# The end of a one-core decoder block: last 512 columns of each side in halves, and one block of the last side scaled by ScalarE and added to residual rows in the output

## The chip, the cores and the metric

The kernel runs on one core of a Trainium2 chip. The metric is the device time of one execution in microseconds (us); the time of a kernel is the median over its runs. A profiled execution gives a span (from the first to the last instruction of the program) and a trace of every engine: PE (TensorE, matmuls; PEld is its weight load), DVE (VectorE), ACT (ScalarE), POOL (GpSimd) and SP (SyncE, which here only issues transfers).

## The reference

One decoder layer over 256 rows of 2048 columns in float32: a mixer (dilated attention and a gated recurrence, not touched here), then a feed-forward part. The end of it is what matters:

```python
h = h + rmsnorm(y @ w_mix_out[layer], norm_mix_post[layer])
a = rmsnorm(h, norm_ffn_pre[layer])
gt, up = jnp.split(a @ w_ffn_gate_up[layer], [D_FF], axis=-1)
ff = (jax.nn.silu(gt) * up) @ w_ffn_down[layer]      # (256, 5632) @ (5632, 2048)
h = h + rmsnorm(ff, norm_ffn_post[layer])
return h
```

The last line needs the mean square of a whole row of ff (2048 columns) before any column of that row can be scaled; the scaled row is then added to h, the residual.

## The kernel before, in words

**Tiling.** The 256 rows are two sides of 128 rows (i = 0, 1; `ov` at line 720 is the output as partition, side, column). The 2048 output columns are four blocks of 512 (j = 0 to 3). The down projection runs as two `Wide` blocks of 1024 columns: the first gives j = 0, 1 and the second, `blocks[-1]`, gives j = 2, 3. Each has 22 steps of 256 rows of the weight. A float32 product is made of three float32r matmuls (high by high, high by low, low by high), all recorded at line 171. In some steps a 2 by 2 block of products is made of seven instead of eight; for that, transfers prepare sums of weights, and `gather` (line 531) folds the banks of the seven into an SBUF tile of four quarters, `e` (`b.rest`), while the last steps go on.

**Order.** Nothing reorders the program: each engine executes its own instructions in the order in which the code emits them (`manual_schedule`), and a framework puts semaphore waits where one engine's instruction needs another's. Transfers are issued by SP (most weight loads, line 302), by POOL (accumulating ones, line 308) and by ACT. A step's weights are loaded, split into high and low parts by ACT (line 399) and DVE (line 407), and multiplied two steps later; SP's next load waits until a buffer is free. At step 6 of `blocks[-1]`, `h_back` (line 1502) has POOL load the residual columns of j = 0, 1, 2 back from memory (`h_t[0]` to `h_t[2]`); `h_t[3]` never left SBUF.

**The end.** The last three steps a, b, c (eight products each, no sevens) are multiplied in an order of their own (lines 1887 to 1897): side 0's j = 2 and 3, then side 1's j = 2 over a, b, c (18 matmuls of 512 columns), then side 1's j = 3 (18 more). After each of these four groups `finish(i, j)` emits

- `down_sum` (line 1614): DVE adds the PSUM bank to its quarter of `e`
- `down_square` (line 1619): ACT squares the quarter and leaves the row sum in a column of `fss`
- `down_gain` (line 1625): DVE multiplies the quarter by the row factor and the gain into `fz[j]`
- for j = 2, `so_far_of` (line 1643): three small DVE operations add the sums of j = 0, 1, 2
- for j = 3, `rsqrt_mean` (line 173: two small ACT and three small DVE operations give `r3`, the row's factor), and then `store` for j = 0 (in two pieces of 128 and 384 columns), 1, 2, 3: DVE makes `fz * r3 + h` (line 1666), and SP or ACT sends it to the output (line 1669).

DVE reads nothing of side 1 before it has stored side 0, since these five operations stand ahead in its order.

Of the kernel before, what the change touches and what calls it, by code (L numbers as in the profile page):

```python
# [16 lines left out]
AF = mybir.ActivationFunctionType  # L17
OP = mybir.AluOpType
# [93 lines left out]
def tile_hybrid_block(ctx: ExitStack, tc: tile.TileContext, t, out):  # L112
    nc = tc.nc
# [11 lines left out]
    def nm(s):  # L125
        serial[0] += 1
        return f"{s}_{serial[0]}"

    def rslot(s):
        return rpool.tile([P, 1024], F32R, tag="r", bufs=16, name=nm(s))  # L130
# [18 lines left out]
    def bank_of(n):  # L149
        return banks(n, 1).tile([P, 512], F32, tag=n, name=nm(n))  # L150

    def pair_of(n):
        return banks(n, 2).tile([P, 2, 512], F32, tag=n, name=nm(n))
# [7 lines left out]
    def p3(s, dtype, n, bufs, tag=None):  # L161
        return pool["now"].tile([P, n], dtype, tag=tag or s, bufs=bufs, name=nm(s))
# [4 lines left out]
    def small(s, n=8, bufs=6):  # L167
        return cpool.tile([P, n], F32, tag=f"small{n}", bufs=bufs, name=nm(s))

    def mm(ps, lhsT, rhs, start, stop):  # L170
        nc.tensor.matmul(ps, lhsT, rhs, start=start, stop=stop, skip_group_check=True)  # L171

    def rsqrt_mean(dst, ss, n, bias=None):

        w = ss.shape[-1]
        v, y, a = (small(s)[:, :w] for s in ("v", "y", "a"))
        bias = bias or (eps[:, 0:1], eps[:, 1:2])  # L180
        nc.scalar.activation(y, ss, AF.Ln, scale=1.0 / n, bias=bias[0])
        nc.scalar.activation(y, y, AF.Exp, scale=-0.5)
        nc.vector.tensor_scalar(v, ss, -0.5 / n, bias[1], op0=OP.mult, op1=OP.add)
        if w == 1:
            nc.vector.scalar_tensor_tensor(out=a, in0=y, scalar=v, in1=y, op0=OP.mult, op1=OP.mult)
        else:
            nc.vector.tensor_mul(a, y, y)
            nc.vector.tensor_mul(a, a, v)
        nc.vector.scalar_tensor_tensor(
            out=dst, in0=a, scalar=1.5, in1=y, op0=OP.add, op1=OP.mult  # L190
        )
# [35 lines left out]
    r2c = cpool.tile([P, 2], F32, name="r2c")  # L227
    r3c = cpool.tile([P, 2], F32, name="r3c")
# [7 lines left out]
    def ptile(s):  # L236
        n = {"early": 4, "middle": 5, "late": 2}[pool["name"]]
        return pool["now"].tile([P, 512], F32, tag="p", bufs=n, name=nm(s))
# [10 lines left out]
    blocks, seq, units, extra = [], [], [], []  # L249
# [221 lines left out]
                    going.remove(g)  # L471
            yield

    def multiply_wide(st, sides=(0, 1), groups=(0, 1)):
        b, i = st.block, st.i
        m, by7 = b.order[i]

        def prod(key, x, w, j, last=False):
            if key not in b.bank:
                side = "aux" if b.flip == (type(key) is not tuple) else "acc"  # L480
                if b.whole:
                    keys = next(k for k in PAIRS if key in k)
                    pair = b.bank[keys] = pair_of(side)
                    b.bank.update((k, pair[:, n, :]) for n, k in enumerate(keys))
                else:
                    b.bank[key] = bank_of(side)
            ps = b.bank[key]
            wh, wl = (v[:, j * 512 : (j + 1) * 512] for v in w)
            mm(ps, x[0], wh, key not in b.open, False)
            mm(ps, x[0], wl, False, False)  # L490
            mm(ps, x[1], wh, False, last)
            b.open.add(key)

        def act_of(s, k):
            return [x[:, s * P : (s + 1) * P] for x in b.xs(2 * m + k)[:2]]

        w = st.parts
        if not by7:
            for s in sides:
                for g in groups:  # L500
                    for k in range(2):
                        prod((s, g), act_of(s, k), w, 2 * g + k, st.last and k == 1)
            return
        w, d, sums = w[:2], w[2:], b.seven(m)
        last = i == b.last7

        go = {
            "o": lambda: prod((0, 1), act_of(0, 1), w, 3, st.last),
            "u": lambda: prod((0, 0), sums(3), w, 1, st.last),
            "t": lambda: prod((1, 1), act_of(1, 1), d, 2, st.last),  # L510
            "1": lambda: prod("p1", act_of(0, 0), w, 2, last),
            "6": lambda: prod("p6", sums(2), d, 0, last),
            "5": lambda: prod("p5", sums(1), d, 1, last),
            "7": lambda: prod("p7", sums(0), w, 0, last),
        }
        seven = [0 <= n < b.steps and b.order[n][1] for n in (i - 1, i + 1)]
        if i == 0:
            steps = "out1657"
        elif st.last:
            steps = "1765out" if seven[0] else "1657out"  # L520
        elif st.between:
            go["x"] = st.between() or (lambda: None)
            steps = "ou1x6t57"
        elif seven[0]:
            steps = "ou17t65"
        else:
            steps = "t65ou17" if seven[1] else "ou1657t"
        for x in steps:
            go[x]()
# [190 lines left out]
    ov = out[0].rearrange("(p b) c -> p b c", b=2)  # L720
# [532 lines left out]
    gates, bases = {}, {}  # L1253
# [32 lines left out]
    h_t, hT, y7 = {}, [], {}  # L1286
# [99 lines left out]
    def from_mix_to_ffn(n):  # L1386
# [41 lines left out]
        high()  # L1428
        mix_square(3, 1, m)
        base = so_far_of(zss[0], 1)  # L1430
        low()
        multiply(f0, (0,))
# [141 lines left out]
    fss, fz, fpost, parts_of, a7 = [], {}, [], {}, {}  # L1574

    def begin_down():
        fss.append(small("fss"))
        for j in range(2):
            fpost.append(rslot("fpost").bitcast(F32))
            nc.scalar.dma_start(  # L1580
                fpost[j],
                t["norm_ffn_post"][:, j * 1024 : (j + 1) * 1024].to_broadcast([P, 1024]),
            )
# [27 lines left out]
    def act(k):  # L1611
        return parts_of[k // 2](k % 2)

    def down_sum(j, i, b):

        f = b.rest[:, 2 * i + j % 2]
        nc.vector.tensor_add(f, b.bank[i, j % 2], f)

    def down_square(j, i, b):
        sq, r2 = fss[0][:, 4 * i + j : 4 * i + j + 1], r2c[:, i : i + 1]  # L1620
        nc.scalar.activation(  # L1621
            ptile("junk"), b.rest[:, 2 * i + j % 2], AF.Square, scale=r2, accum_out=sq
        )

    def down_gain(j, i, b):
        if i == 0:
            fz[j] = p3("fz", F32, 1024, 4, "so").rearrange("p (b c) -> p b c", b=2)
        nc.vector.scalar_tensor_tensor(
            out=fz[j][:, i, :], in0=b.rest[:, 2 * i + j % 2], scalar=r2c[:, i : i + 1],
            in1=fpost[j // 2][:, (j % 2) * 512 : (j % 2 + 1) * 512],  # L1630
            op0=OP.mult, op1=OP.mult,
        )

    def evac_down(b):
        parts = [(j, i) for i in range(2) for j in range(2)]
# [4 lines left out]
            down_gain(j, i, b)  # L1640
            yield

    def so_far_of(ss, i):

        b = small("base")
        nc.vector.tensor_reduce(
            b[:, 0:1], ss[:, 4 * i : 4 * i + 3], op=OP.add, axis=mybir.AxisListType.X
        )
        nc.vector.tensor_scalar(b[:, 0:1], b[:, 0:1], 1.0 / D, EPS, op0=OP.mult, op1=OP.add)
        nc.vector.tensor_scalar(b[:, 1:2], b[:, 0:1], -0.5, None, op0=OP.mult)  # L1650
        return b[:, 0:1], b[:, 1:2]

    def finish(i, j):

        b = blocks[-1]
        down_sum(j, i, b)
        down_square(j, i, b)
        down_gain(j, i, b)
        if j == 2:
            bases[i] = so_far_of(fss[0], i)  # L1660
            return
        sq, r3 = fss[0][:, 4 * i + 3 : 4 * i + 4], r3c[:, i : i + 1]

        def store(j, lo=0, hi=512, eng=nc.sync):
            z = fz[j][:, i, lo:hi]
            nc.vector.scalar_tensor_tensor(  # L1666
                out=z, in0=z, scalar=r3, in1=h_t[j][:, i, lo:hi], op0=OP.mult, op1=OP.add
            )
            eng.dma_start(ov[:, i, j * 512 + lo : j * 512 + hi], z)

        rsqrt_mean(r3, sq, D, bases[i])
        store(0, 0, 128)
        store(0, 128, 512, nc.scalar)
        store(1)
        store(2, eng=nc.scalar)
        store(3)


    w_in = t["w_in"][0]
# [69 lines left out]
    w = w_gu = t["w_ffn_gate_up"][0]  # L1749
# [31 lines left out]
    if len(H7) > 4:  # L1781
        first_j = [b for b in blocks if b.w is w_gu and type(b) is Wide][0]
        first_j.at[4] = more_sums
        blocks[-1].at[6] = h_back

    later = []

# [42 lines left out]
    for n, st in enumerate(seq):  # L1830
        b, i = st.block, st.i
# [55 lines left out]
    a, b, c = seq[-3:]  # L1887
    for g in range(2):
        for st in (a, b):
            multiply_wide(st, (0,), (g,))  # L1890
    for g in range(2):
        multiply_wide(c, (0,), (g,))
        finish(0, 2 + g)
    for g in range(2):
        for st in (a, b, c):
            multiply_wide(st, (1,), (g,))
        finish(1, 2 + g)


# [49 lines left out]
```

## Time and profile before

| | |
|---|---|
| median of 3 runs | 1674.45 us (1674.42 to 1674.69) |
| the profiled execution | 1675.0 us, its span 1673.2 us |
| PE busy | 1661.8 us, 99% of the span |
| DVE busy | 1477.7 us, 88% |
| ACT, POOL busy | 960.5 us (57%), 230.4 us (14%) |
| last matmul ends | 1664.6 us after the span's start |

PE is busy nearly throughout, so up to 1664.6 us the kernel lasts as long as its matmuls. The 8.6 us behind them belong to the last block's norm, the stores and their landing. Views used below: the page of the run; the chain of waits (what each piece of work waited for, followed back from the end); the groups of instructions by form; the timeline (one row for each instruction, or run of like ones: start, duration, engine, line); the busy time by windows; and the issues of transfers with their time from issue to landing.

### The profile page before, as it was taken

Reading aid. Unit: us, or ns where it says so; the run is one execution under the profiler, and the core shown is the slowest. Engines: PE = TensorE matmul, PEld = TensorE weight load, DVE = VectorE, ACT = ScalarE, POOL = GpSimd, SP = SyncE. Lnnn points to the kernel's source line nnn. Section 1 sums busy time; section 2 is a strip of 40 time slices with the busy share of each in tenths; the row PEclk is TensorE's granted clock in tenths of the full one; section 3 lists DMA queues with packets and bytes.
Section 4 is the critical chain, followed back from the end, with each engine's and each line's share of the span. In section 5 each row is a group of like instructions: output and inputs, shape, how many; then the busy total and the mean of one; then the engine's idle time right before and its main releaser. Section 6 shows DMA issues by size and latency. Waiting matters only on the chain.

```text
span 1673.2 us, 21505 instructions
## 1 busy us (share of the span) xinstructions
PE 1661.8 (99%) x8028; PEld 1390.4 (83%) x8028; DVE 1477.7 (88%) x1512; ACT 960.5 (57%) x959; POOL 230.4 (14%) x309
## 2 busy tenths in 40 slices
PE   9999999999999999999999999999999999999997
PEld 7888888888888888888888888888888888888886
DVE  6799999999987998867668888999999999899988
ACT  6566555565665444445445565666666666666664
POOL 0001111111003311313311010111111111000100
PEclk9999999999999999999999999999999999999999
DMA  8888888998769997969988857998988989887892
GB/s 283 268 261 258 269 244 264 277 289 274 234 204 316 313 268 219 279 209 303 297 249 250 279 187 245 274 277 273 282 280 268 283 268 278 255 256 236 258 307 103
DMA packets 235705, 436.56 MB, mean 261 GB/s; under 512 B 15408, under 2 KB 65632, under 8 KB 235600
## 3 DMA queue, kind: packets, MB, share of 16 engines
q1 hardware_dynamic: 195920, 345.94, 61.3%
q0 software_dynamic: 37056, 83.32, 22.7%
q10 hardware_dynamic: 2624, 5.92, 1.0%
q8 instruction: 63, 1.03, 0.3%
q14 instruction: 42, 0.34, 0.1%
HBM read 422.01 MB, written 52.43 MB: 284 GB/s over the span
## 4 chain that ended last, share of the span: by engine, by line
PE 93%; DVE 3%; DMA 2%; issue 1%; ACT 1%; SPq 0%; DVEq 0%; POOLq 0%; ACTq 0%
PE acc L171 52%; PE aux L171 39%; DMA raw<-in_w_mix_out 2%; DVE wl L407 1%; PE aux L1033 0%; DMA x<-in_x 0%; ACT w L399 0%; DVE dl L430 0%; PE acc L1534 0%; DVE fz L1666 0%; PE aux L651 0%; PE aux L1534 0%; DVE w L361 0%; ACT junk L1621 0%; ACT dh L427 0%
## 5 line engine op out<-in xcount | busy, mean ns | idle before, releaser
L399 ACT ACTIVATE w<-raw 128x2048 fp32r<-128x2048 f32 x220 | 420.8, 1914 | 228.3 <-PE acc L171 62.0
L407 DVE TENSOR_TENSOR wl<-raw,w 128x2048 fp32r<-128x2048 f32 x220 | 500.8, 2286 | 22.6 <-ACT w L399 21.1
L171 PE MATMUL acc<-xT,w 128*128 128x512 f32 (+1 forms) x1536 | 279.0, 339 | 0.0
L171 PEld LDWEIGHTS acc<-xT,w 128*128 128x128 f32 x1536 | 234.6, 188 | 33.3 <-DVE w L361 0.2
L360 ACT ACTIVATE w<-raw 128x1024 fp32r<-128x1024 f32 (+1 forms) x159 | 166.7, 1052 | 160.0 <-PE acc L171 107.6
L361 DVE TENSOR_TENSOR w<-raw,w 128x1024 fp32r<-128x1024 f32 (+1 forms) x159 | 193.1, 1216 | 66.7 <-ACT w L360 66.0
L427 ACT ACTIVATE dh<-sum 128x1536 fp32r<-128x1536 f32 x113 | 168.5, 1491 | 141.5 <-PE acc L171 59.4
L430 DVE TENSOR_TENSOR dl<-sum,dh 128x1536 fp32r<-128x1536 f32 x113 | 198.0, 1752 | 16.7 <-ACT dh L427 16.3
L171 PE MATMUL aux<-w,xT 128*128 128x512 f32 x534 | 174.1, 389 | 0.0
L171 PE MATMUL acc<-w,hT 128*128 128x512 f32 x504 | 152.9, 391 | 0.0
L171 PE MATMUL acc<-w,xT 128*128 128x512 f32 x422 | 125.4, 393 | 0.3 <-DVE w L361 0.2
L171 PE MATMUL aux<-w,hT 128*128 128x512 f32 x368 | 122.9, 390 | 0.0
L171 PEld LDWEIGHTS aux<-w,xT 128*128 128x128 f32 x534 | 100.2, 188 | 20.6
L171 PEld LDWEIGHTS acc<-w,hT 128*128 128x128 f32 x504 | 94.0, 188 | 19.8 <-DVE w L361 0.4
L171 PE MATMUL aux<-wl,xT 128*128 128x512 f32 x267 | 103.9, 389 | 0.0
L308 POOL DMA_DIRECT2D raw<-in_w_ffn_gate_up x48 | 42.3, 881 | 377.0 <-DMA raw<-in_w_ffn_gate_up 144.9
L171 PE MATMUL acc<-dh,so 128*128 128x512 f32 x260 | 92.9, 391 | 0.0
L171 PEld LDWEIGHTS acc<-w,xT 128*128 128x128 f32 x422 | 78.3, 188 | 17.4 <-DVE w L361 1.2
L308 POOL DMA_DIRECT2D raw<-in_w_in x43 | 37.9, 882 | 395.3 <-DMA raw<-in_w_in 243.9
L171 PE MATMUL aux<-w,a 128*128 128x512 f32 x260 | 83.3, 389 | 0.0
L171 PE MATMUL aux<-w,so 128*128 128x512 f32 x210 | 81.8, 389 | 0.0
L171 PE MATMUL acc<-w,so 128*128 128x512 f32 x210 | 81.8, 389 | 0.0
(340 smaller groups left out, 3018.7 us busy)
## 6 DMA issues: line engine op xcount, KB each, us to landing
raw<-in_w_in SPq DMA_DIRECT2D x271, 512.0 KB, 6.1
raw<-in_w_ffn_gate_up SPq DMA_DIRECT2D x176, 512.0 KB, 4.8
raw<-in_w_ffn_down SPq DMA_DIRECT2D x88, 512.0 KB, 5.5
sum<-ready SPq DMA_DIRECT2D x25, 768.0 KB, 6.8
ready<-in_w_ffn_gate_up POOLq DMA_DIRECT2D x72, 256.0 KB, 7.3
raw<-in_w_mix_out SPq DMA_DIRECT2D x32, 512.0 KB, 6.7
ready<-ready POOLq DMA_DIRECT2D x50, 256.0 KB, 7.1
raw<-in_w_ffn_gate_up POOLq DMA_DIRECT2D x48, 256.0 KB, 6.0
```

The source lines that it names most:

```text
L171: nc.tensor.matmul(ps, lhsT, rhs, start=start, stop=stop, skip_group_check=True)
L308: nc.gpsimd.dma_start(raw[:, :512], rows, accum_op=OP.add)
L360: nc.scalar.activation(wh[:, k], raw[:, k], AF.Copy)
L361: nc.vector.tensor_sub(wl[:, k], raw[:, k], wh[:, k].bitcast(F32))
L399: nc.scalar.activation(hi, raw, AF.Copy)
L407: nc.vector.tensor_sub(lo, raw, hi.bitcast(F32))
L427: nc.scalar.activation(hi, flat, AF.Copy)
L430: nc.vector.tensor_sub(lo, flat, hi.bitcast(F32))
```

## The change

Three things, all in the end.

1. The j = 3 group of each side is multiplied in two halves of 256 columns: `multiply_wide` gets a `cut`, and `finish` is called for each half. The sum of squares gets 8 columns for each side, and `so_far_of` now adds four of them (j = 0, 1, 2 and the first half of 3) behind the first half.
2. For side 1, block j = 2 leaves `store`: ACT scales `fz[2]` by `r3` into the tile that held the residual, and POOL sends it with an accumulating transfer to the output, where the residual rows of that block were put earlier.
3. These rows are put there by `h_first`, a plain transfer on SP at step 10 of `blocks[-1]`. Side 1's last store moves from SP to ACT.

```diff
-    def multiply_wide(st, sides=(0, 1), groups=(0, 1)):
+    def multiply_wide(st, sides=(0, 1), groups=(0, 1), cut=slice(0, 512)):
...
-            ps = b.bank[key]
-            wh, wl = (v[:, j * 512 : (j + 1) * 512] for v in w)
+            ps = b.bank[key][:, cut]
+            wh, wl = (v[:, j * 512 : (j + 1) * 512][:, cut] for v in w)
...
-    def down_sum(j, i, b):
-
-        f = b.rest[:, 2 * i + j % 2]
-        nc.vector.tensor_add(f, b.bank[i, j % 2], f)
+    def down_sum(j, i, b, lo=0, hi=512):
+
+        f = b.rest[:, 2 * i + j % 2, lo:hi]
+        nc.vector.tensor_add(f, b.bank[i, j % 2][:, lo:hi], f)
...
+    def h_first():
+
+        nc.sync.dma_start(ov[:, 1, 1024:1536], h_t[2][:, 1, :])
...
-    def finish(i, j):
+    def finish(i, j, lo=0, hi=512):
 
         b = blocks[-1]
-        down_sum(j, i, b)
-        down_square(j, i, b)
-        down_gain(j, i, b)
+        down_sum(j, i, b, lo, hi)
+        down_square(j, i, b, lo, hi)
+        down_gain(j, i, b, lo, hi)
         if j == 2:
-            bases[i] = so_far_of(fss[0], i)
             return
-        sq, r3 = fss[0][:, 4 * i + 3 : 4 * i + 4], r3c[:, i : i + 1]
+        if lo == 0:
+            bases[i] = so_far_of(fss[0], i, 4, 8)
+            return
+        sq, r3 = fss[0][:, 8 * i + 4 : 8 * i + 5], r3c[:, i : i + 1]
...
         rsqrt_mean(r3, sq, D, bases[i])
+        if i == 1:
+            z = h_t[2][:, 1, :]
+            nc.scalar.activation(z, fz[2][:, 1, :], AF.Copy, scale=r3)
+            nc.gpsimd.dma_start(ov[:, 1, 1024:1536], z, accum_op=OP.add)
         store(0, 0, 128)
         store(0, 128, 512, nc.scalar)
         store(1)
-        store(2, eng=nc.scalar)
-        store(3)
+        if i == 0:
+            store(2, eng=nc.scalar)
+        store(3, eng=nc.scalar if i else nc.sync)
...
         blocks[-1].at[6] = h_back
+        blocks[-1].at[10] = h_first
...
-    for g in range(2):
-        multiply_wide(c, (0,), (g,))
-        finish(0, 2 + g)
-    for g in range(2):
+    multiply_wide(c, (0,), (0,))
+    finish(0, 2)
+    for lo in (0, 256):
+        multiply_wide(c, (0,), (1,), slice(lo, lo + 256))
+        finish(0, 3, lo, lo + 256)
+    for st in (a, b, c):
+        multiply_wide(st, (1,), (0,))
+    finish(1, 2)
+    for lo in (0, 256):
         for st in (a, b, c):
-            multiply_wide(st, (1,), (g,))
-        finish(1, 2 + g)
+            multiply_wide(st, (1,), (1,), slice(lo, lo + 256))
+        finish(1, 3, lo, lo + 256)
```

What the built programs hold at the two places. First PE, inside side 1's j = 3 group (bank `acc_12472`), where step c of one pass ends. Before, it is the end of the matmuls:

```order
L171 MATMUL acc_12472<-w_13199,a_13197 128x512
L171 MATMUL acc_12472<-wl_13200,a_13197 128x512
L171 MATMUL acc_12472<-w_13199,a_13197 128x512 x2
L171 MATMUL acc_12472<-wl_13200,a_13197 128x512
L171 MATMUL acc_12472<-w_13199,a_13197 128x512
```

Now, at the end of the first half and the start of the second (what an instruction waits for stands in brackets):

```order
L171 MATMUL acc_12472<-wl_13201,a_13198 128x256
L171 MATMUL acc_12472<-w_13200,a_13198 128x256 x2
L171 MATMUL acc_12472<-wl_13201,a_13198 128x256
L171 MATMUL acc_12472<-w_13200,a_13198 128x256
L171 MATMUL acc_12472<-w_13133,a_13131 128x256 [waits DVE_49]
L171 MATMUL acc_12472<-wl_13134,a_13131 128x256
L171 MATMUL acc_12472<-w_13133,a_13131 128x256 x2
```

The same steps are now gone through twice at 256 columns, and the first matmul of the second pass waits for DVE; the count it waits for is that of the add (line 1617) of the first half out of the same bank. Side 0's j = 3 group (bank `acc_12464`) has the same wait, with all of side 1's matmuls behind it.

Second DVE, from side 1's first add to its `r3`. Before:

```order
L1617 TENSOR_TENSOR e_13191<-acc_12525,e_13191 128x512 [waits PE_49]
L1628 SCALAR_TENSOR_TENSOR fz_13237<-e_13191,r2c,fpost_11552 128x512 [waits DVE_49]
L1646 TENSOR_REDUCE base_13294<-fss_11549 128x1 [waits Activation_49]
L1649 TENSOR_SCALAR base_13294<-base_13294 128x1 [waits DVE_49]
L1650 TENSOR_SCALAR base_13294<-base_13294 128x1 [waits DVE_49]
L1617 TENSOR_TENSOR e_13191<-acc_12472,e_13191 128x512 [waits PE_49]
L1628 SCALAR_TENSOR_TENSOR fz_13252<-e_13191,r2c,fpost_11552 128x512 [waits DVE_49]
L183 TENSOR_SCALAR v_13320<-fss_11549,base_13294 128x1 [waits Activation_49]
```

Now:

```order
L1617 TENSOR_TENSOR e_13192<-acc_12525,e_13192 128x512 [waits PE_49]
L1630 SCALAR_TENSOR_TENSOR fz_13238<-e_13192,r2c,fpost_11552 128x512 [waits DVE_49]
L1617 TENSOR_TENSOR e_13192<-acc_12472,e_13192 128x256 [waits PE_49]
L1630 SCALAR_TENSOR_TENSOR fz_13249<-e_13192,r2c,fpost_11552 128x256 [waits DVE_49]
L1652 TENSOR_REDUCE base_13327<-fss_11549 128x1 [waits Activation_49]
L1655 TENSOR_SCALAR base_13327<-base_13327 128x1 [waits DVE_49]
L1656 TENSOR_SCALAR base_13327<-base_13327 128x1 [waits DVE_49]
L1617 TENSOR_TENSOR e_13192<-acc_12472,e_13192 128x256 [waits PE_49]
L1630 SCALAR_TENSOR_TENSOR fz_13249<-e_13192,r2c,fpost_11552 128x256 [waits DVE_49]
L183 TENSOR_SCALAR v_13353<-fss_11549,base_13327 128x1 [waits Activation_49]
```

There is one add and one gain more, and the three small operations, which wait for ACT's square, have moved from ahead of the one add of j = 3 to between its two halves.

More of the change, by code (lines that the diff above doesn't have):

```diff
@@ L1576, in begin_down @@
     def begin_down():
-        fss.append(small("fss"))
+        fss.append(small("fss", 16, 1))
         for j in range(2):
@@ L1612, in act, with down_square, down_gain @@
         return parts_of[k // 2](k % 2)
-    def down_sum(j, i, b):
-        f = b.rest[:, 2 * i + j % 2]
-        nc.vector.tensor_add(f, b.bank[i, j % 2], f)
-    def down_square(j, i, b):
-        sq, r2 = fss[0][:, 4 * i + j : 4 * i + j + 1], r2c[:, i : i + 1]
+    def down_sum(j, i, b, lo=0, hi=512):
+        f = b.rest[:, 2 * i + j % 2, lo:hi]
+        nc.vector.tensor_add(f, b.bank[i, j % 2][:, lo:hi], f)
+    def down_square(j, i, b, lo=0, hi=512):
+        at = 8 * i + j + (lo > 0)
+        sq, r2 = fss[0][:, at : at + 1], r2c[:, i : i + 1]
         nc.scalar.activation(
-            ptile("junk"), b.rest[:, 2 * i + j % 2], AF.Square, scale=r2, accum_out=sq
+            ptile("junk")[:, lo:hi], b.rest[:, 2 * i + j % 2, lo:hi], AF.Square, scale=r2, accum_out=sq
         )
-    def down_gain(j, i, b):
-        if i == 0:
+    def down_gain(j, i, b, lo=0, hi=512):
+        if j not in fz:
             fz[j] = p3("fz", F32, 1024, 4, "so").rearrange("p (b c) -> p b c", b=2)
+        at = j % 2 * 512
         nc.vector.scalar_tensor_tensor(
-            out=fz[j][:, i, :], in0=b.rest[:, 2 * i + j % 2], scalar=r2c[:, i : i + 1],
-            in1=fpost[j // 2][:, (j % 2) * 512 : (j % 2 + 1) * 512],
+            out=fz[j][:, i, lo:hi], in0=b.rest[:, 2 * i + j % 2, lo:hi], scalar=r2c[:, i : i + 1],
+            in1=fpost[j // 2][:, at + lo : at + hi],
             op0=OP.mult, op1=OP.mult,
         )
+    def h_first():
+        nc.sync.dma_start(ov[:, 1, 1024:1536], h_t[2][:, 1, :])
     def evac_down(b):
@@ L1641, in evac_down, with so_far_of @@
             yield
-    def so_far_of(ss, i):
+    def so_far_of(ss, i, n=3, per=4):
         b = small("base")
         nc.vector.tensor_reduce(
-            b[:, 0:1], ss[:, 4 * i : 4 * i + 3], op=OP.add, axis=mybir.AxisListType.X
+            b[:, 0:1], ss[:, per * i : per * i + n], op=OP.add, axis=mybir.AxisListType.X
         )
```

## The prediction

> **What bounds the kernel now.** I read the page first:
>
> ```profile
> span 1673.2 us, 21505 instructions
> PE 1661.8 (99%) x8028; PEld 1390.4 (83%) x8028; DVE 1477.7 (88%) x1512; ACT 960.5 (57%) x959; POOL 230.4 (14%) x309
> ```
>
> PE sets the time until it ends, at 1664.6. The change touches only the last stretch, so next I read the chain of waits there (start, duration, engine, output, line):
>
> ```profile
> 1655.12 0.70 DVE e L1617
> 1655.84 0.82 ACT junk L1621 x2
> 1656.69 0.17 DVE base L1646
> 1658.77 0.30 ACT y L181
> 1659.78 2.87 DVE fz L1666 x5
> 1662.65 0.61 DVE e L1617
> 1663.28 0.82 ACT junk L1621 x2
> 1664.13 0.17 DVE base L1646
> 1664.66 0.67 DVE e L1617
> 1665.36 0.82 ACT junk L1621 x2
> 1666.21 0.30 ACT y L181
> 1667.02 0.17 DVE r3c L189
> 1667.22 0.35 DVE fz L1666
> 1668.10 1.99 DVE fz L1666 x3
> ```
>
> From 1655.12 on it holds DVE and ACT alone. Side 0's five stores (2.87 us) end at 1662.65, and only then does DVE take side 1's j = 2, although PE goes on. So DVE's list already decides in these last 10 us; PE, which ends at 1664.60, ends level with DVE's small operations (1664.66). Behind `r3` at 1667.19 come the stores, one each 0.66 us (1.99 for three), the last transfer at 1670.1 and its landing. The issue view of the last transfers (KB, us from issue to landing):
>
> ```profile
> out_dram<-fz SPq DMA_DIRECT2D x2, 256.0 KB, 2.1
> out_dram<-fz ACTq DMA_DIRECT2D x1, 256.0 KB, 2.1
> ```
>
> So the last landing is at 1670.1 + 2.1 = 1672.2, and the span ends 1.0 us later. Two windows behind the last matmul (behind the five engines stand PE's granted clock, the share of the transfer engines, GB/s):
>
> ```profile
> 1664.60:1669.60 5.00, 0.00 (x0) 0.00 (x0) 4.45 (x11) 1.31 (x4) 0.00 (x0) 1.00 0.16 52
> 1670.00:1673.20 3.20, 0.00 (x0) 0.00 (x0) 0.09 (x1) 0.00 (x0) 0.00 (x0) 0.50 0.54 202
> ```
>
> 202 GB/s at a share of 0.54 is 374 GB/s for stores at full load, 0.70 us for 256 KB.
>
> **The change, part by part.**
>
> *Half sizes.* The halves' operations are not in this trace, but operations of 256 columns are (groups by form; mean ns before the last bar):
>
> ```profile
> L562 DVE TENSOR_TENSOR s<-act 128x256 f32<-128x256 f32 x6 | 2.5, 417 | 0.0
> L1354 ACT ACTIVATE zg<-zg,rzc 128x256 f32<-128x256 f32 x5 | 2.6, 517 | 0.0
> L1568 ACT ACTIVATE e<-e,r2c 128x512 f32<-128x512 f32 x20 | 13.3, 709 | 1.0 <-DVE e L552 1.0
> ```
>
> An add of half size takes 0.42 us instead of 0.69. ACT, also with a scale from memory, is 0.19 shorter at 256 columns than at 512 (709 less 517), so the square with its read of the sum takes 0.82 - 0.19 = 0.63. For matmuls, 8 us of an earlier stage, in which 22 of the 47 were 256 wide:
>
> ```profile
> 552.00:560.00 8.00, 8.00 (x47) 6.93 (x47) 7.90 (x13) 3.58 (x5) 1.21 (x2) 1.00 1.09 323
> L171 PE MATMUL acc<-xT,w 128*128 128x256 f32 x22 | 4.3, 277 | 0.0
> 1654.69 0.62 PE L171 MATMUL acc<-w,a 128*128 128x512 f32 x2
> ```
>
> A 512-wide one starts 0.227 us after the last (two in 0.62 at 0.39 each), so 25 of them take 5.67 and leave 0.106 for each narrow one. I take half of 0.227, 0.114; the halves then cost PE nothing in themselves. A narrow result is there 0.28 after its start.
>
> *The new waits of PE.* The first matmul of each second half waits for DVE's add out of the first half. An earlier stall of PE on DVE shows what a release costs (timeline; idle time and releaser in brackets):
>
> ```profile
> 1431.31 1.75 DVE L430 TENSOR_TENSOR dl<-sum,dh 128x1536 fp32r<-128x1536 f32 x1
> 1433.12 0.50 PE L171 MATMUL aux<-dl,so 128*128 128x512 f32 x1 [0.24 <-DVE dl L430]
> ```
>
> PE starts 0.06 after DVE's end (1433.06), and the first matmul takes 0.11 more than the usual 0.39.
>
> The Trainium skill, PSUM — Partial Sum Buffer, section "PSUM bank collisions raise a hardware error", says that accesses of two engines to PSUM are to be kept apart by bank (and by group of 32 partitions), disjoint columns or not. By that rule the wait cannot be had away within one bank and the sum below stands; without it the sum would be the third rival's. No row here shows a bank shared in halves.
>
> *Side 0.* The add of j = 2 stays at 1655.12. Its gain starts at 1655.84, and the next DVE operation 0.66 later: the half add runs 1656.50 to 1656.92. PE has made its first half (six matmuls from 1654.92) by 1655.60 and stands until 1656.98, 1.4 us; behind the waiting matmul stands the whole of side 1. Its second half takes 6 x 0.114 + 0.11, to 1657.77. The timeline has the add behind the small operations before:
>
> ```profile
> 1657.14 0.68 DVE L1617 TENSOR_TENSOR e<-acc,e 128x512 f32<-128x512 f32 x1
> ```
>
> It starts 0.45 behind the first of the three (1656.69). So now: the half's square 1656.95 to 1657.58, the three from 1657.61, the second add 1658.06 to 1658.48, its square to 1659.14, and ACT's logarithm at 1659.17 instead of 1658.77: the stores of side 0, and all behind them on DVE, are 0.40 late.
>
> *Side 1.* DVE's add of j = 2 comes at 1662.56 + 0.40 = 1662.96 (PE is through with it by 1657.77 + 18 x 0.227 + 0.16 = 1662.0), the gain at 1663.68, the half add 1664.34 to 1664.76. PE has ended its first half at 1663.9 and stands 0.9 us, to 1664.82. Second half: 18 x 0.114, plus 0.11, plus the 0.16 by which a result trails the next start: 1667.15 instead of 1664.60. Meanwhile DVE's small operations end before 1666. So PE now decides: add 1667.19 to 1667.61, square to 1668.27, logarithm at 1668.30 instead of 1666.21. **`r3` is 2.09 us late**, at 1669.28. The shorter last add and square (0.27 + 0.19) are in this already.
>
> *The stores.* One DVE operation fewer on side 1: the last store ends 0.66 earlier relative to `r3`, at 1670.09 + 2.09 - 0.66 = 1671.52, and lands 2.1 later, at 1673.64: 1.4 us later than now.
>
> *The accumulating transfer.* ACT scales from 1669.31 for 0.71 (the 709 ns row), to 1670.02. Then POOL issues. What that costs is shown by its other accumulating transfers of 256 KB (line 308), all into SBUF; these rows show a wait for one load, and the two ends of the landing time:
>
> ```profile
> 1599.11 1.52 SPq L302 DMA_DIRECT2D raw<-in_w_ffn_down  x2
> raw<-in_w_ffn_down SPq DMA_DIRECT2D x1, 512.0 KB, 7.9
> 1607.72 0.89 POOL L308 DMA_DIRECT2D raw<-in_w_ffn_down  x1 [8.83 <-DMA raw<-in_w_ffn_down]
> 437.24 0.86 POOL L308 DMA_DIRECT2D raw<-in_w_in  x1 [20.16 <-DVE e L552]
> raw<-in_w_in POOLq DMA_DIRECT2D x1, 256.0 KB, 4.0
> DMA to landing us min/median/max: 3.9/6.1/8.5
> ```
>
> The load issued at 1599.11 landed 7.9 later, at 1607.0; POOL's issue started 0.7 behind it. So here it starts at 1670.7. Landing takes 4.0 us in the quiet stretch at 437, 3.9 at best, 6.1 in the median, under the weight stream. The bounds are 2.1 (a plain store out of the same SBUF, above) and 6.1. I take 4.4: near the quiet end, since weights no longer stream, but two stores of 256 KB (issued at 1670.9 and 1671.5) are still on the way when its packets come, and it writes to memory rather than SBUF. It lands at 1675.1, after the last plain store, **2.9 us later than the last landing now**.
>
> The Trainium skill, DMA: Bandwidth & Descriptors, section "Anatomy of one DMA — SWDGE (gpsimd) path", fits such a transfer as about 2.0 us plus bytes over 436 GB/s; that is an estimate of 2.6 us for 256 KB, the transfer would be over before the last store, and the sum would be the first rival's. The trace's fastest, 3.9, disagrees for transfers into SBUF; no row here shows one into the output.
>
> *`h_first`.* One 256 KB transfer on SP near 1605, 0.7 us of the transfer engines by the rate above. Queued behind it are the last loads of weights. SP's own waits after 1600 are:
>
> ```profile
> SPq L302 <- DVE wl L407: 25.7, 7, 4.8
> 1624.09 1.92 ACT L399 ACTIVATE w<-raw 128x2048 fp32r<-128x2048 f32 x1 [1.56 <-PE acc L171]
> 1627.91 1.49 ACT L427 ACTIVATE dh<-sum 128x1536 fp32r<-128x1536 f32 x1 [1.90 <-PE acc L171]
> ```
>
> SP waits for free buffers 25.7 us in seven times, and ACT idles over 1 us ahead of the splits, so I put it at 0. If that cover were gone it would cost its 0.7 us at most. The wider `fss` costs nothing: no instruction.
>
> *Sum.* 2.09 for `r3`, and behind it 0.8 more than now for the path through ACT and POOL: 2.9. On the profiled execution, 1675.0 (span 1673.2 and 1.8 around it), that gives 1677.9; it was 0.55 above the median, so on the median of 1674.45 it is **1677.3 us**, 0.17% up. I call 0.2%, 3.35 us or 1677.8, the least that a measurement of this kernel tells from no change.
>
> **The rivals.**
>
> 1. The accumulating transfer is hidden: it lands within 2.9 us of its issue, before 1673.6. For it, plain stores land in 2.1; against it, no accumulating one in the trace landed in under 3.9. The last store then ends the kernel: +1.4, **1675.9**. Chance 0.11.
> 2. The other side, slower by over 0.2%: its packets come only after the queued stores and it lands as under the weight stream, 6.1 after 1670.7, at 1676.8: +4.6, **1679.0**. For it, the median; against it, the transfer engines then carry only 0.7 MB. It decides from a landing time of 4.9 us (1675.55). Chance 0.23.
> 3. The change's halves overlap after all: PE does not stand, the second add comes right behind the small operations, at 1665.90, and the logarithm at 1667.01, so `r3` is only 0.80 late: 1.29 less than the sum, **1676.0**. Against it stand the two waits in PE's order. If in addition the transfer is hidden and side 0 costs nothing, the end gains the 0.66 and 0.46: 1673.3. Chance 0.05 for both, and 0.02 for a gain of over 0.2% from any cause.
> 4. PE's clock falls in its two new stands and the second halves run at half of it: 2 us more behind the second stand, **1679.4**, and more if side 1's whole group is hit. Against it, the granted clock is still 1.00 over the 5 us behind the last matmul and 0.50 only later (the two windows above); the stands are 1.4 and 0.9. Chance 0.03.
>
> **How the numbers follow.** The forecast has 0.56. The range runs from the hidden transfer to the loaded one, 1675.7 to 1679.0; it leaves out half of rivals 2, 3 and 4, and little else. Faster needs an end of under 1671.1, which no case gives: 0.02. Slower: rivals 2 and 4, and 0.04 of the forecast in which `r3` or the landing is half a microsecond later: 0.30. The same: 0.68.
>
> **What would show it.** In the profile of the changed kernel, PE has two idle stretches, near 1656 and 1664, both ended by DVE's line 1617, of 1.4 and 0.9 us; the second add of side 1 is released by PE, near 1667.2; `r3` is there near 1669.3; POOL's one transfer is issued near 1670.7 and lands last. Wrong would be: no idle time of PE (the waits met early), an `r3` before 1668.5, a landing of the POOL transfer ahead of the last store or after 1676, or a loss of PE before 1650, which would be `h_first`.

## The result, and the profile after

The changed kernel takes **1680.34 us** in the median of seven runs (1678.28 to 1682.51), the kernel before 1674.45 in its seven (1673.89 to 1677.3): a ratio of 1.0029, with a 95% interval of 1.0020 to 1.0039. (The ratio is not the quotient of the two medians, which is 1.0035, or 5.9 us.) It is slower, by 3.3 to 6.5 us. The forecast was 1677.3 and its range ended at 1679.0. A second comparison, further down, gave 1.0025 (1.0016 to 1.0034).

The page of the changed kernel; its profiled execution took 1680.21 us:

```profile
span 1678.4 us, 21568 instructions
PE 1663.5 (99%) x8052; PEld 1392.2 (83%) x8052; DVE 1477.7 (88%) x1515; ACT 962.0 (57%) x964; POOL 230.8 (14%) x310
```

PE's share is 99% as before, so the page does not show where the time went. The chain of waits does, from the same place on as before (start, duration, engine, output, line; DVE's adds are line 1617 in both kernels):

```profile
1655.97 0.70 DVE e L1617
...
1660.10 0.30 ACT y L181
...
1661.11 2.87 DVE fz L1674 x5
1663.98 0.61 DVE e L1617
1664.62 0.75 DVE fz L1630
1665.37 0.34 DVE e L1617
1665.76 2.42 PE acc L171 x18
...
1668.20 0.43 DVE e L1617
...
1669.36 0.30 ACT y L181
...
1670.17 0.17 DVE r3c L189
```

The new piece is PE's, 18 narrow matmuls behind DVE's half add: PE waits for DVE, then DVE for PE. Both stands of PE, in the timeline (idle time and releaser in brackets):

```profile
1657.83 0.39 PE L171 MATMUL acc<-w,a 128*128 128x256 f32 x1 [1.20 <-DVE e L1617]
1665.76 0.39 PE L171 MATMUL acc<-w,a 128*128 128x256 f32 x1 [0.69 <-DVE e L1617]
```

Behind `r3` stand ScalarE's scaling, GpSimd's issue, and the two plain issues on ACT's queue, the second of them block 3's and the last of all (its row ends at 1672.94, and an issue takes 0.34, so it starts at 1672.60):

```profile
1670.37 0.72 ACT L1682 ACTIVATE h<-fz,r3c 128x512 f32<-128x512 f32 x1 [0.48 <-DVE r3c L189]
1671.28 1.66 ACTq L1677 DMA_DIRECT2D out_dram<-fz  x2
1671.49 0.88 POOL L1683 DMA_DIRECT2D out_dram<-h  x1 [43.29 <-ACT h L1682]
```

The first rows of the issue view of the last 10 us (KB each, us from issue to landing):

```profile
out_dram<-h POOLq DMA_DIRECT2D x1, 256.0 KB, 5.4
out_dram<-fz SPq DMA_DIRECT2D x1, 256.0 KB, 2.5
out_dram<-fz ACTq DMA_DIRECT2D x1, 256.0 KB, 4.8
```

The accumulating transfer lands at 1671.49 + 5.4 = 1676.9. The last to land is a plain store of 256 KB: 1672.60 + 4.8 = 1677.4, where such a store took 2.1 before. The span ends 1.0 us later, as before.

**Three parts.** The span is 5.2 us longer (1678.4 against 1673.2). Of that, 0.85 is lost before DVE's add of side 0's j = 2 (1655.97 against 1655.12). From this add to the end of `r3` it is 14.37 us (1670.17 + 0.17 - 1655.97) where it was 12.07 (1667.02 + 0.17 - 1655.12): **2.30**. From there to the span's end it is 8.06 where it was 6.01: **2.05**.

The 0.85 does not come from the change's instructions. Both kernels execute the same ones in the same order until `h_first` is issued at 1606 us, and the loss is older. Between 1180 and 1200, the row of before and then that of the changed kernel (busy time of PE, PEld, DVE, ACT, POOL, then PE's clock, transfer share, GB/s):

```profile
1180.00:1200.00 20.00, 20.00 (x94) 16.54 (x93) 18.34 (x14) 13.38 (x11) 1.75 (x2) 1.00 0.90 271
```

```profile
1180.00:1200.00 20.00, 19.36 (x90) 15.63 (x89) 17.31 (x13) 13.25 (x10) 1.74 (x2) 1.00 0.89 271
...
1185.90 1.92 ACT L399 ACTIVATE w<-raw 128x2048 fp32r<-128x2048 f32 x1 [2.45 <-DMA raw<-in_w_ffn_gate_up]
```

PE made four matmuls fewer (0.9 us at 0.227 each) because a load of weights came late, 400 us ahead of the first changed instruction. Where such losses lie and how large they are differs from one profile to the next, as the experiments show.

### The profile page after: what moved, and what is told of

The parts are those of the page before. It is cut to its first block, busy times and chain, and to the rows that moved or that the text cites. A ratio compares the mean times of both kernels' runs of the same rounds, so it can differ in the third digit from the quotient of the medians.

```text
span 1678.4 us, 21568 instructions
## 1 busy us (share of the span) xinstructions
PE 1663.5 (99%) x8052; PEld 1392.2 (83%) x8052; DVE 1477.7 (88%) x1515; ACT 962.0 (57%) x964; POOL 230.8 (14%) x310
## 3 DMA queue, kind: packets, MB, share of 16 engines
q10 hardware_dynamic: 2624, 5.92, 1.1%
## 4 chain that ended last, share of the span: by engine, by line
PE 94%; DVE 3%; DMA 1%; issue 1%; ACT 1%; DVEq 0%; ACTq 0%; POOLq 0%
PE acc L171 53%; PE aux L171 38%; DVE wl L407 1%; DMA raw<-in_w_ffn_gate_up 1%; PE aux L1033 0%; DMA sum<-ready 0%; PE aux L651 0%; PE acc L1534 0%; DVE fz L1674 0%; PE aux L1534 0%; DVE w L361 0%; PE aux L639 0%; DVE dl L430 0%; ACT w L399 0%; ACT dh L427 0%
```

## The experiments

Each timed kernel was run beside the kernel before, which took 1675.33 to 1677.43 us in these comparisons and 1674.45 in the first; the absolute times in the expectations start from 1674.45 and are to be read as differences from it. Since the time ahead of the tail varies by more than the effects, the table also gives what one profile shows of the tail alone: from the start of DVE's add of side 0's j = 2 (A) to the end of `r3`, and from there to the end of the span; "tail" is the sum of both stretches less the 18.08 of before. Each row is one profile. How far such a figure can be trusted is shown by those that should agree: 4.35 and 4.23 for the change, -0.07 for the early rows alone. Ratios have their 95% intervals.

| kernel | A | A to `r3` | `r3` to end | tail | ratio of times |
|---|---|---|---|---|---|
| before | 1655.12 | 12.07 | 6.01 | 0 | 1 |
| the change | 1655.97 | 14.37 | 8.06 | +4.35 | 1.0029 (1.0020 to 1.0039) |
| the change again | 1657.69 | 14.37 | 7.94 | +4.23 | 1.0025 (1.0016 to 1.0034) |
| halves alone | 1656.78 | 14.38 | 5.94 | +2.24 | 1.0018 (1.0010 to 1.0027) |
| accumulation alone | 1655.85 | 12.07 | 7.88 | +1.87 | 1.0010 (1.0001 to 1.0019) |
| early rows alone | 1658.19 | 12.07 | 5.94 | -0.07 | 1.0001 (0.9992 to 1.0009) |
| plain transfer from GpSimd | 1657.11 | 14.37 | 5.92 | +2.21 | 1.0014 (1.0005 to 1.0023) |
| halves, own bank | 1654.90 | 13.50 | 6.00 | +1.42 | 1.0010 (1.0001 to 1.0018) |
| halves on side 0 | 1655.65 | 13.62 | 5.93 | +1.47 | one run |
| halves on side 1 | 1658.12 | 13.88 | 6.00 | +1.80 | one run |
| accumulation last | 1658.92 | 12.07 | 9.01 | +3.00 | one run |
| GpSimd adds | 1656.56 | 12.06 | 6.58 | +0.56 | 1.0002 (0.9992 to 1.0011) |
| small store last | 1654.68 | 12.06 | 6.06 | +0.04 | 0.9994 (0.9985 to 1.0003) |

### Halves alone

```diff
-        if i == 1:
-            z = h_t[2][:, 1, :]
-            nc.scalar.activation(z, fz[2][:, 1, :], AF.Copy, scale=r3)
-            nc.gpsimd.dma_start(ov[:, 1, 1024:1536], z, accum_op=OP.add)
...
-        if i == 0:
-            store(2, eng=nc.scalar)
-        store(3, eng=nc.scalar if i else nc.sync)
+        store(2, eng=nc.scalar)
+        store(3)
...
-        blocks[-1].at[10] = h_first
```

> The halves alone; side 1's four blocks are stored as before, and the early residual rows and the accumulating transfer are left out. Theory (PE stands twice at the bank that it shares with DVE): r3 comes 14.3 to 14.4 us after the add of side 0's j = 2 instead of 12.07, and the time is 2.3 us up, about 1676.7. Rival (the halves cost little, nearly all of the 5.9 us comes from the transfer): r3 at most 13 after that add, under 1675.4. If a part of the loss lies ahead of the tail and comes with the halves, 1677.5.

`r3` came 14.38 us behind A, the time was 0.18% up (1.7 to 4.5 us). The whole shift of `r3` in the changed kernel belongs to the halves:

```profile
1656.78 0.69 DVE L1617 TENSOR_TENSOR e<-acc,e 128x512 f32<-128x512 f32 x1 [1.68 <-PE acc L171]
...
1671.00 0.16 DVE L189 SCALAR_TENSOR_TENSOR r3c<-a,y 128x1 f32<-128x1 f32 x1
```

### The accumulating transfer alone

The kernel before, plus `h_first`, ScalarE's scaling and the accumulating transfer; side 1's last store goes from ACT, as in the change.

> The early residual rows and the accumulating transfer alone; all blocks 512 wide as before. Theory (the accumulating packets take 178 ns instead of 84 and hold up the last plain store): r3 as before, 12.1 after the add of side 0's j = 2, the last landing 7.0 after r3 instead of 5.0, the time 2.0 us up, 1676.5. Rival 1 (the early rows cost the 0.85 us that was lost ahead of the tail as well): 1677.3. Rival 2 (the long landings came only with the halves): the last landing at most 5.5 after r3, under 1675.

`r3` was where it had been, the end 1.87 us later behind it. The long landings are there without the halves:

```profile
out_dram<-h POOLq DMA_DIRECT2D x1, 256.0 KB, 5.1
out_dram<-fz SPq DMA_DIRECT2D x1, 256.0 KB, 2.6
out_dram<-fz ACTq DMA_DIRECT2D x1, 256.0 KB, 4.6
```

2.24 and 1.87 make 4.11 of the 4.35 and 4.23: but for 0.1 to 0.2 us, the two parts of the change add up.

### The early rows alone

```diff
         blocks[-1].at[6] = h_back
+        blocks[-1].at[10] = h_first
```

> Before, with the residual rows of side 1's block 2 written into the output early (256 KB on SP's queue near 1606 us); the plain store of that block overwrites them later. Theory (it is covered; the 0.85 us ahead of the tail is the spread of single executions): no change, 1674.0 to 1674.9. Rival (it delays the last weights): 0.7 to 0.9 up, 1675.2 or more, and the add of side 0's j = 2 late by as much in a PE wait behind 1606.

The tail is as before, the ratio 1.0001. This one profile reached A 3.07 us later than the profile of before, and again not at the changed place. Its window, and the one of before:

```profile
400.00:450.00 50.00, 47.58 (x223) 39.12 (x222) 44.99 (x36) 27.06 (x23) 6.02 (x8) 1.00 0.80 246
```

```profile
400.00:450.00 50.00, 50.00 (x237) 41.88 (x236) 48.17 (x40) 29.15 (x23) 6.02 (x8) 1.00 0.86 264
```

2.4 us of idle PE at 400 to 450 us, at 246 GB/s instead of 264, and 1150 us ahead of `h_first`. The expectation's second half, that a late A would speak for the rival, was a bad test by itself: A varies from 1654.7 to 1658.9 over the thirteen profiles, and the kernels without `h_first` vary by 3.4 of it. It has to be asked where the time was lost. From 1500 us to 1655 us PE does not idle in this profile, nor in the one of before or in the other five with `h_first` (155.00 us busy in each), so the early rows, issued at 1606 to 1609, cost nothing ahead of A:

```profile
1500.00:1655.00 155.00, 155.00 (x685) 128.42 (x684) 148.83 (x151) 102.04 (x93) 12.17 (x15) 1.00 0.79 246
```

### A plain transfer from GpSimd

```diff
-            nc.gpsimd.dma_start(ov[:, 1, 1024:1536], z, accum_op=OP.add)
+            nc.gpsimd.dma_start(ov[:, 1, 1024:1536], z)
```

> The change with a plain transfer from GpSimd's queue in the place of the accumulating one, so that the residual of that one block is left out of the sum. Theory (accumulation makes it slow): packets of about 85 ns, landing 2.1 to 3 us after the issue, the last plain store lands 2.1 to 2.5 after its own, the last landing 4.4 to 4.8 after r3, the time about 1676.2. Rival (GpSimd's queue makes it slow, whatever it carries): landing 4 to 5.4 after the issue, the last landing 5.5 to 7 after r3, 1677.3 to 1678.8.

The output of this kernel lacks the residual of that block. First the issue, then the landings:

```profile
1672.60 0.58 POOL L1683 DMA_DIRECT2D out_dram<-h  x1 [43.53 <-ACT h L1682]
```

```profile
out_dram<-h POOLq DMA_DIRECT2D x1, 256.0 KB, 2.9
out_dram<-fz SPq DMA_DIRECT2D x1, 256.0 KB, 2.7
out_dram<-fz ACTq DMA_DIRECT2D x1, 256.0 KB, 2.6
```

With the same queue, the same place and the same bytes, the landing falls from 5.4 to 2.9 us, that of the last plain store from 4.8 to 2.6, and the end behind `r3` is level with before (5.92 and 6.01). The last landing is 4.9 behind `r3`, a little later than the 4.4 to 4.8 expected. So it is the accumulation that costs, not GpSimd's queue, and not the last store's move from SP to ACT either, which this kernel has too. In the trace's records of packets the accumulating transfer of the changed kernel is 128 packets of 2048 bytes with a median of 178 ns, over 2.9 us (1673.5 to 1676.4). The last plain store's packets take 84 ns in the median and begin only at 1675.0, 2.4 us after its issue; before, the last store's began 0.9 after its issue. The plain transfer from GpSimd has 64 packets of 4096 bytes and 159 ns, not the 85 ns expected: per byte it is as quick as the plain stores.

The Trainium skill, DMA: Bandwidth & Descriptors, section "Anatomy of one DMA — SWDGE (gpsimd) path", whose fit gave an estimate of 2.6 us, is near this plain transfer (2.9) and not the accumulating one (5.1 to 5.4 here). The same page of the Trainium skill, section "Queues, rings and completion order", says that an engine drains a whole packet of descriptors from one ring before it turns to the next ring; the late first packets of the plain store fit that, but no row names the engine of each packet, so this way of holding up is not shown.

### The accumulating transfer behind the plain ones

The accumulation alone, with ScalarE's scaling and the transfer emitted after the last plain store.

> The early rows and the accumulating transfer without the halves, as in the run of these two alone, but ScalarE scales its block only after it has issued the last plain store, so that the accumulating packets come behind the plain ones. Theory (packets of different queues wait for each other on the transfer engines; whoever comes second is held up): the last plain store lands 2.0 to 2.2 after its issue again (4.6 when it came second), the accumulating transfer 3.9 to 4.6 after its own (5.1 to 5.4 among the plain ones). Rival (accumulation into the output's memory is slow in itself): 5 or more after its issue with nothing else on the way.

```profile
1674.77 0.88 POOL L1685 DMA_DIRECT2D out_dram<-h  x1 [44.56 <-ACT h L1684]
```

```profile
out_dram<-h POOLq DMA_DIRECT2D x1, 256.0 KB, 3.9
out_dram<-fz ACTq DMA_DIRECT2D x1, 256.0 KB, 2.0
```

Now the last plain store lands in 2.0 us, and the accumulating transfer in 3.9, the figure of the fastest one into SBUF in the trace before; so nothing here shows that writing to the output is slower in itself. Among plain stores it took 1.2 to 1.5 more, and the plain store issued behind it lost 2.5 to 2.8. This also gives a floor: scaling (0.72), issue (0.40 behind it) and 3.9 make 5.0 us behind `r3`, and the four blocks stored by DVE had landed 5.0 behind `r3` before. By these rows the replacement could not have gained even with the transfer engines to itself.

### Halves without PE's wait

```diff
-            ps = b.bank[key][:, cut]
+            if cut.start:
+                key = (key, "hi")
+            ps = b.bank[key][:, cut]
...
+        key = (i, j % 2)
+        if lo:
+            key = (key, "hi")
+        elif hi < 512:
+            hi = 512
         f = b.rest[:, 2 * i + j % 2, lo:hi]
-        nc.vector.tensor_add(f, b.bank[i, j % 2][:, lo:hi], f)
+        nc.vector.tensor_add(f, b.bank[key][:, lo:hi], f)
```

A pair of PSUM banks that is free by then holds the last products of both second halves (its allocation is left out here). DVE's add for the first half is now 512 wide, and the stores are those of before.

> The halves without PE's waits: the last products of each second half go to a PSUM bank of their own, and DVE's add for the first half is 512 wide (it takes the older sums of the second half along). Stores as before, no accumulating transfer. Theory (PE's stands are only what shows; DVE's list, one operation longer on each side, decides behind them): PE ends near 1664.6 plus the lateness ahead of the tail, r3 still 1.3 to 1.6 us later behind the add of side 0's j = 2 than before (13.4 to 13.7 instead of 12.06). Rival (the shared bank is the whole loss): r3 at most 12.3 behind it, or sooner than before.

PE no longer stands and ends 9.82 us behind A (9.48 before), and yet `r3` is 1.43 late. PE's last matmul, and then DVE's rows on side 1:

```profile
1664.44 0.28 PE L171 MATMUL aux<-w,a 128*128 128x256 f32 x1
```

```profile
1663.10 0.68 DVE L1624 TENSOR_TENSOR e<-acc,e 128x512 f32<-128x512 f32 x1
1663.82 0.75 DVE L1637 SCALAR_TENSOR_TENSOR fz<-e,r2c,fpost 128x512 f32<-128x512 f32 x1
1664.49 0.68 DVE L1624 TENSOR_TENSOR e<-acc,e 128x512 f32<-128x512 f32 x1
1665.20 0.48 DVE L1637 SCALAR_TENSOR_TENSOR fz<-e,r2c,fpost 128x256 f32<-128x256 f32 x1
...
1666.29 0.41 DVE L1624 TENSOR_TENSOR e<-aux,e 128x256 f32<-128x256 f32 x1
```

There is hardly a gap: an add and a gain more on DVE stand ahead of the last add, which starts at 11.39 behind A (9.51 before) although its products were ready at 9.8. Taking PE's wait away gave back 0.9 of the 2.3 us, after paying for the wider add (0.68 instead of 0.42 on each side); the rest is the price of more operations on an engine whose list is full.

### One side in halves

Halves on side 0 alone, and on side 1 alone; the other side's j = 3 as before.

> Halves on side 0 alone, stores as before. Theory: PE stands 1.4 us once and ends 1.5 late, with its 512-wide results; r3 comes 13.5 to 13.6 behind the add of side 0's j = 2 (12.06 before, 14.37 with both sides in halves). Rival (only the last half on side 1 counts, since DVE's list hides the rest): 12.1 to 12.5.

> Halves on side 1 alone, stores as before. Theory: PE is through with its first half at 1662.5, stands 1.9 us until DVE's half add, and r3 comes 13.8 to 13.9 behind the add of side 0's j = 2, so that the two sides' losses (1.5 and 1.8) do not add up to the 2.3 of both. Rival (they add up): 12.06 + 2.31 less what side 0 alone costs, 12.8 to 12.9.

13.62 and 13.88, as the first theory had them (13.62 is 0.02 over its range). Alone, side 0 costs 1.55 and side 1 1.81, but both together 2.30 and not 3.36. A reading that fits the sum: with both, side 0 hands on only the 0.48 by which its norm is late (1660.10 - 1655.97 = 4.13 from A to its logarithm, 3.65 before), and 1.81 + 0.48 = 2.29. Its own stand of PE (1.20) makes the second one shorter, which alone is 1.75 and with both 0.69:

```profile
1667.42 0.39 PE L171 MATMUL acc<-w,a 128*128 128x256 f32 x1 [1.75 <-DVE e L1617]
```

### GpSimd adds the residual in SBUF

The kernel before, no halves; on side 1 ScalarE scales block 2, GpSimd adds the residual, and a plain transfer stores it:

```diff
+        if i == 1:
+            z = fz[2][:, 1, :]
+            nc.scalar.activation(z, z, AF.Copy, scale=r3)
+            nc.gpsimd.tensor_add(z, z, h_t[2][:, 1, :])
```

> Before, without halves and early rows; ScalarE scales side 1's block 2 in place, GpSimd adds the residual in SBUF and a plain transfer stores it. Theory (the idea of taking one of DVE's last operations away is right, its transfer was not): GpSimd's add takes about 1.5 us (its 256-wide ones take 0.77), the last landing comes 4.3 to 4.6 after r3 instead of 5.0, the time 0.4 to 0.7 us less than before. Rival (DVE or GpSimd is slowed while both work): 5.0 or more after r3.

```profile
1668.66 3.27 DVE L1666 SCALAR_TENSOR_TENSOR fz<-fz,r3c,h 128x128 f32<-128x128 f32 x4
...
1669.46 1.26 POOL L1675 TENSOR_TENSOR fz<-fz,h 128x512 f32<-128x512 f32 x1 [40.76 <-ACT fz L1674]
```

GpSimd's add is faster than expected, but DVE's four stores take 3.27 us here and 2.21 in the changed kernel. In the records, the one that starts with GpSimd's add at 1669.46 lasts until 1671.27, 1.81 instead of 0.75. The rival holds: the last landing is 5.5 behind `r3`, and in place of a gain of one DVE operation (0.66) the tail of this profile is 0.56 longer. The times alone do not show it (0.9992 to 1.0011). The Trainium skill, SBUF — State Buffer, section "Who interferes with whom", names a port pair that DVE and GpSimd share under an exclusive lock, so that one blocks and does not merely slow down. The trace agrees in the main: DVE's operation ends 0.55 behind GpSimd's, where a whole one begun at GpSimd's end would take 0.66 to 0.75.

### The small store last

On side 1 three blocks of 512 columns, then 384 and 128 of block 3.

> Before, with side 1's 128 columns stored last in the place of first (three blocks of 512, then 384 columns of block 3, then its last 128); no halves, no transfer of another kind. DVE's work is the same. Theory (behind r3 the end is DVE's last store and the landing of what it wrote, and 64 KB land in 1.54 us where 256 KB take 2.07): the last landing 4.5 to 4.6 after r3 instead of 5.0, the time 0.4 to 0.5 us less, which the times can hardly show. Rival (the transfers are bound by the rate of the engines, and start too late): 5.0 or more after r3, the time the same or more.

```profile
out_dram<-fz SPq DMA_DIRECT2D x1, 64.0 KB, 2.0
```

The rival holds: 64 KB land in 1.5 us in front of the others and in 2.0 behind them, and the last landing is 5.0 behind `r3` as before. No version here beats the kernel before by what can be measured.

### The change once more

> The changed kernel once more, unaltered, beside the kernel before. Theory (2.3 us from the halves and 2.0 from the transfer; whatever else the first comparison showed is the spread of single executions ahead of the tail): 4.3 us up, ratio near 1.0026. Rival (another 0.8 to 1.6 us belongs to the change, ahead of the tail): 5.2 to 5.9 up, ratio 1.0031 to 1.0035.

1680.01 against 1675.33 us beside it, a ratio of 1.0025, or 4.2 us (2.7 to 5.7). That is the 4.3 of the tail and not 5.9; the rival's lower end, 5.2, lies within the interval, and the times alone do not exclude it. What speaks against it is that the instructions up to `h_first` are those of before, and that PE is busy for the full 155 us from 1500 to 1655 in every profile with `h_first`.

## Why the prediction was wrong, step by step

**What bounds it, and the stands of PE: right.** Both stands were there, ended by line 1617 (1.20 and 0.69 of idle time; counted as the forecast did, from when the next matmul could have started, 1.35 and 0.85, where 1.4 and 0.9 were forecast). Side 0's logarithm was 0.48 late (forecast 0.40), PE decided behind the second stand, and `r3` came 2.30 late where 2.09 was forecast. The 0.21 are small pieces: 0.08 on side 0, 0.01 more up to PE's second start, 0.07 in the second half (2.44 us to the last add, not 2.37) and 0.05 from that add to the logarithm. That `h_first` is covered was borne out. That the halves cost PE nothing in themselves was nearly so: a narrow matmul starts 0.12 after the last, not 0.114, and where PE did not stand at all it ended 0.34 later (9.82 and 9.48).

**The landing of the accumulating transfer: mis-sized.** "I take 4.4: near the quiet end" measured 5.4 and 5.2 in the two profiles of the change and 5.1 in that of the accumulation alone. Alone it lands in 3.9. The text named the two plain stores that would still be on the way and gave them 0.5; they cost 1.2 to 1.5. The issue, on the other hand, came 0.40 behind ScalarE and not 0.7; that figure was taken from a wait for a load. By its landing this is the second rival (it decides from 4.9), at a chance of 0.23, but not by its mechanism: that had the accumulating packets wait behind the queued stores, and here they began 1.5 us ahead of the last plain store's.

**The last plain store: the step that failed.** "and lands 2.1 later, at 1673.64" took the row of a store among plain stores and left it at that once the accumulating transfer stood beside it. It took 4.8 and was the last to land. The forecast asked what the plain stores do to the new transfer and not what that does to them. The end came 2.05 us later behind `r3` than before, where 0.8 was forecast. Of these 1.25 us, 0.75 are the late landing of the accumulating transfer (with that alone the end would be 0.5 earlier), and the last 0.5 the plain store that landed behind it.

**Sum and range.** 2.09 + 0.8 = 2.9 became 2.30 + 2.05 = 4.35; on the median of before that is 1678.8, inside the range and over the bound of 0.2%. The first comparison's 1680.34 lies 1.5 above, and that takes it out of the range. It is made of 0.85 lost ahead of A in the profiled execution, 0.55 by which the profiled execution of before lies over its median, and 0.13 by which that of the change lies under its own: spread of single executions, ahead of the tail where a profile shows it. The range put this spread at nothing; the three runs shown, 0.27 us apart, suggested none, but seven of the same kernel spread over 3.4, and its medians in the five comparisons over 3.0. It took both to leave the range: the mis-sized sum alone stays within it, and so would the forecast's 1677.3 with 1.5 on top.

**The other rivals.** The first, a landing within 2.9 us, did not happen; only a plain transfer from GpSimd's queue landed so soon. The third, that PE does not stand, was built with the bank of its own: `r3` 1.43 late instead of the 0.80 in the text. Its price assumed half adds on DVE; with a bank of its own the first add is 512 wide again, 0.27 more on each side, which makes 1.34. The fourth, a falling clock, did not happen: PE's granted clock (the third figure from the end) is 1.00 in the windows of both stands and is lower only behind the last matmul, which ended at 1668.2.

```profile
1655.00:1660.00 5.00, 3.81 (x23) 3.23 (x22) 3.54 (x9) 1.95 (x6) 0.00 (x0) 1.00 0.01 3
1664.60:1669.60 5.00, 2.88 (x22) 2.47 (x21) 3.16 (x9) 2.26 (x7) 0.00 (x0) 1.00 0.20 76
1669.60:1673.20 3.60, 0.00 (x0) 0.00 (x0) 2.58 (x6) 0.98 (x3) 0.88 (x1) 0.74 0.32 115
```

## What to carry to other kernels

Before an operation is taken off a busy engine, work out the shortest path of its replacement to the end: here scaling, issue and the fastest landing came to the same 5.0 us as the four stores that they were to relieve. Ask of every range whether it has a term for how far whole executions of the kernel differ. When a slower kind of transfer joins others, price both directions: what the others do to it, and what it does to those issued behind it. Cutting a result in halves to overlap two engines needs idle time on the engine that takes the halves; here its list was full, and the extra operations came out at the end, with PE's wait and without it.

## What the runs showed of the hardware that was not expected

- An accumulating transfer of 256 KB from SBUF to the output landed in 3.9 us alone and in 5.1 to 5.4 among plain stores; its packets of 2048 bytes took 178 ns in the median, plain ones 84. A plain store of 256 KB issued 1.1 us behind it on another queue landed in 4.6 to 4.8 instead of 2.0 to 2.1.
- GpSimd's issue took 0.88 us for the accumulating transfer and 0.58 for a plain one, and began about 0.4 behind the ScalarE instruction that it waited for.
- A tensor add of GpSimd over 128 by 512 took 1.26 us, and a DVE operation that started with it took 1.81 instead of 0.75.
- Executions of one kernel differ by several us (the kernel before: 1673.9 to 1680.3 over all its runs). In the two profiles read for it, the loss was idle PE behind late weights: 0.6 us of it between 1180 and 1200, 2.4 between 400 and 450.
